# An mLSTM whose gate rows reach all partitions through memory and not through selector products

## The chip, the cores and the metric

The kernel runs on one core of a Trainium2 chip. The metric is device time in microseconds (us) of one execution; the kernel before has a median of 1518.31 us over three runs.

## The reference, cut to what matters

Two layers, each a mixer and a mixture of experts, on 512 tokens of width 1024. The mixer has two branches that read the same modulated rows, an mLSTM and a windowed attention. The part of the mLSTM that matters here:

```
# per head (4 heads, keys of 64, values of 128), causal, over 512 tokens
i, f      = gate columns of the input projection
b         = cumsum(log_sigmoid(f))
# state form, chunk by chunk, with a running maximum m (the stabilizer)
decay     = exp(b_last + m - m_new)
C_new     = decay * C + fresh * C_loc
# output of a token t of a chunk
W[s, t]   = exp(i_s - b_s + b_t - m_t)  for s <= t, else 0
num       = (W * (q k^T / 8)) v  +  exp(b_t + m - m_t) * (q / 8) C
out       = sigmoid(o) * rmsnorm(num / max(|den|, ...)) * w_mnorm
```

The kernel takes chunks of 128 tokens, so there are four of them, cc = 0 to 3.

## The kernel before

Large products run on TensorE (PE) in three passes each: every weight chunk is split into a high part (`wh`, by ScalarE, ACT) and a low part (`wl`, by VectorE, DVE), and the rows into `hh` and `hl`; a `unit` of the input projection is 24 products of 128x512. The units are v, the mLSTM's q and k (with a convolution `cv` on DVE and a silu `qk` on ACT), o (tiles `tok`, later `so`), the attention's `qa`, and so on. The pieces of the mLSTM are put between these units: `ml_prep` after 5 units of v and o, `ml_qi` and `ml_a(0)` between the units of o, then for each chunk `ml_b`, `ml_c`, `ml_a` of the next chunk, and `ml_d`.

The three gate rows are computed with one head per partition, on 4 partitions: `Mm` (4x512, the stabilizer), `inn` (4x512, the factor of the carried state) and `dec` (4x4, the decay of the state). They are needed on all 128 partitions. Before, a product with a 0/1 matrix does that: `sel` (4 x 4 x 128) and `sel2` (4 x 2 x 128), built by `selectors` in each layer. `ml_prep` makes `decp` and copies it to `decb`; `ml_qi` makes `innb` and multiplies q with it into `qi`; `ml_a` makes `mlW`, four blocks of 128x128, each a product of `sel` with `Mm` plus a product of `identb` (a bf16 identity) with `maskbig`, a 128x128 tile that is 1e30 above the diagonal. ACT then takes the exponential of `mlW` into `mlWs`, DVE multiplies it with the scores `mlS` into `mlSW`, and PE uses that in `mlN`. `ml_c` ends in `hm`, which `ml_d` turns on PE (`hmT`).

Every engine takes its instructions in the order of its own list. A list scheduler makes these lists from the program when the kernel is built, by its own estimates; so a change at one place may move instructions elsewhere. Weights come by the queue of SyncE (SP) into a ring of buffers (`raw`); among them is the modulation's weight `w_ada`, which DVE adds up into `acc` (`Ada.emit`), one 1 MB chunk in two instructions. A chunk's load starts when the instruction that read the buffer's former content has ended. GpSimd (POOL) has a DMA queue of its own, for small loads, for `bscr` and `brev` (a relative-position bias that goes to memory and is read back broadcast) and for gathers.

## Time and profile before

| | |
|---|---|
| runs | 1517.87, 1518.31, 1520.58 us; median 1518.31 us |
| profiled execution | its span from first to last instruction, 1523.3 us, is the one time known of it |
| span against the median | 5.0 us (0.33%) longer |
| PE | 1447.8 us busy (95%), 88% of the chain that ended last |
| DVE, ACT, POOL | 1094.8 us (72%), 759.6 us (50%), 220.3 us (14%) busy |
| the mLSTM in time | layer 0 from about 76 to 170 us, layer 1 from about 797 to 905 us of the span |

A view by windows gives busy time of each engine in a stretch and the clock granted to TensorE there; 1.00 is 2.4 GHz and 0.5 is 1.2 GHz. A row of the timeline gives start, duration, engine, line, operation, output and inputs, shape and count, and in square brackets how long the engine had been idle and what ended that. Products are pipelined, so one is issued before the last has ended, and the distance of two starts says more than a duration.

### The profile page before, as it was taken

To read this page: it belongs to the slowest core of one execution; us is meant where nothing else is said; L and a number is where in the kernel's file an instruction comes from. 1 tells how busy PE (TensorE), PEld (TensorE's weight loads), DVE (VectorE), ACT (ScalarE), POOL (GpSimd) and SP (SyncE) were. 2 spreads that over 40 slices of the span, in tenths; PEclk is the share of its full clock that TensorE was granted. 3 is DMA by queue.
4 is the path that set the end of the run, shared out by engine and by line. 5 is a ranking of instruction groups with operands and counts; after the bars stand their busy time and mean duration, and the time that the engine had idled before them with its cause. 6 is when DMAs were issued, how large, how long until landed. Compare 5 with 4: busy or idle time off the path is not lost.

```text
span 1523.3 us, 18682 instructions
## 1 busy us (share of the span) xinstructions
PE 1447.8 (95%) x6551; PEld 1085.9 (71%) x6551; DVE 1094.8 (72%) x2011; ACT 759.6 (50%) x1276; POOL 220.3 (14%) x266
## 2 busy tenths in 40 slices
PE   3999999999979999999899999999997999999995
PEld 2877777778867677677577777777886767767753
DVE  6776666767679777687766646656867977778757
ACT  4354444544356566566355334544434656656643
POOL 6500010010131111110230000001003111111023
PEclk9998999999989999999999899999998999999998
DMA  9564474575669999994735334446566999999582
GB/s 330 204 197 139 156 259 139 194 212 207 229 238 339 364 354 357 351 369 168 284 129 163 113 96 134 149 148 163 204 242 229 332 357 355 350 358 370 198 312 96
DMA packets 167779, 365.09 MB, mean 240 GB/s; under 512 B 11830, under 2 KB 42798, under 8 KB 167417
## 3 DMA queue, kind: packets, MB, share of 16 engines
q1 hardware_dynamic: 152928, 327.71, 62.2%
q0 software_dynamic: 14032, 33.93, 6.5%
q10 hardware_dynamic: 712, 2.14, 0.4%
q8 instruction: 55, 0.90, 0.2%
q14 instruction: 52, 0.42, 0.1%
HBM read 348.89 MB, written 29.41 MB: 248 GB/s over the span
## 4 chain that ended last, share of the span: by engine, by line
PE 88%; DVE 7%; issue 1%; DMA 1%; ACT 1%; another core or an unknown queue 0%; POOL 0%; SPq 0%; DVEq 0%; ACTq 0%; POOLq 0%
PE down L1449 9%; PE winT L112 7%; PE winT L113 7%; PE winT L114 7%; PE gate L114 4%; PE gate L112 4%; PE gate L113 4%; PE up L113 4%; PE up L114 4%; PE up L112 4%; PE out L112 2%; PE out L114 2%; PE out L113 2%; PE tok L114 2%; PE PV L909 2%; PE sc L867 2%
## 5 line engine op out<-in xcount | busy, mean ns | idle before, releaser
L1397 ACT CAST wh<-raw 128x1024 fp32r<-128x1024 f32 x248 | 258.2, 1049 | 214.5 <-PE gate L114 166.9
L1398 DVE TENSOR_TENSOR wl<-raw,wh 128x1024 fp32r<-128x1024 f32 x248 | 299.4, 1221 | 68.0 <-ACT wh L1397 64.4
L112 PE MATMUL winT<-hh,wh 128*128 128x512 f32 x432 | 177.3, 411 | 0.0
L113 PE MATMUL winT<-hl,wh 128*128 128x512 f32 x432 | 173.5, 402 | 0.0
L114 PE MATMUL winT<-hh,wl 128*128 128x512 f32 x432 | 173.0, 401 | 0.0
L1449 PE MATMUL down<-raw,aT 128*128 128x512 f32 x320 | 141.2, 593 | 3.0 <-ACT aT L1432 3.0
L479 ACT CAST wh<-raw 128x1024 fp32r<-128x1024 f32 (+1 forms) x59 | 54.4, 930 | 144.3 <-PE winT L113 99.2
L274 DVE SCALAR_TENSOR_TENSOR acc<-raw,cs,acc 128x1024 f32<-128x1024 f32 x70 | 89.6, 1280 | 35.3 <-DMA raw<-in_w_ada_dram 34.6
L112 PE MATMUL gate<-wh,XTh 128*128 128x512 f32 x256 | 109.9, 429 | 3.3 <-ACT XTh L1389 2.6
L1449 PEld LDWEIGHTS down<-raw,aT 128*128 128x128 f32 x320 | 59.2, 190 | 69.9 <-issue 65.5
L112 PEld LDWEIGHTS winT<-hh,wh 128*128 128x128 f32 x432 | 83.2, 193 | 29.9 <-issue 10.5
L113 PE MATMUL gate<-wl,XTh 128*128 128x512 f32 x256 | 103.1, 403 | 0.5 <-DVE wl L1398 0.5
L113 PE MATMUL up<-wl,XTh 128*128 128x512 f32 x256 | 101.5, 397 | 0.8 <-DVE wl L1398 0.8
L114 PE MATMUL gate<-wh,XTl 128*128 128x512 f32 x256 | 101.6, 397 | 0.2
L112 PE MATMUL up<-wh,XTh 128*128 128x512 f32 x256 | 101.2, 395 | 0.0
L114 PE MATMUL up<-wh,XTl 128*128 128x512 f32 x256 | 101.1, 395 | 0.0
L114 PEld LDWEIGHTS winT<-hh,wl 128*128 128x128 f32 x432 | 83.1, 192 | 19.8
L113 PEld LDWEIGHTS winT<-hl,wh 128*128 128x128 f32 x432 | 83.0, 192 | 18.1 <-DVE hl L459 0.3
L480 DVE TENSOR_TENSOR wl<-raw,wh 128x1024 fp32r<-128x1024 f32 (+1 forms) x57 | 60.7, 1067 | 44.1 <-ACT wh L479 43.8
L1358 POOL DMA_INDIRECT X<-h2d,gidx x30 | 38.9, 1296 | 281.8 <-PE XT L1370 258.8
L1451 DVE TENSOR_TENSOR Y<-down,g 128x512 f32<-128x512 f32 x60 | 40.4, 687 | 50.8 <-PE down L1449 50.8
L1452 POOL DMA_INDIRECT y2d<-Y,slot x30 | 37.8, 1261 | 225.9 <-DVE Y L1451 180.4
(490 smaller groups left out, 3053.7 us busy)
## 6 DMA issues: line engine op xcount, KB each, us to landing
raw<-in_w_down_e_dram SPq DMA_DIRECT2D x64, 1024.0 KB, 7.7
raw<-in_w_gate_e_dram SPq DMA_DIRECT2D x62, 1024.0 KB, 8.1
raw<-in_w_up_e_dram SPq DMA_DIRECT2D x62, 1024.0 KB, 8.5
raw<-in_w_ada_dram SPq DMA_DIRECT2D x40, 1024.0 KB, 5.3
raw<-in_w_in_dram SPq DMA_DIRECT2D x30, 1024.0 KB, 6.2
sch<-in_w_ada_dram SPq DMA_DIRECT2D x32, 256.0 KB, 6.3
raw<-in_w_out_dram SPq DMA_DIRECT2D x8, 1024.0 KB, 5.1
yk<-y2d SPq DMA_DIRECT2D x8, 1024.0 KB, 15.0
```

The lines of the kernel that those rows point to most:

```text
L112: T.matmul(o, lh, rh, start=start, stop=False)
L113: T.matmul(o, lh, rl, start=False, stop=False)
L114: return T.matmul(o, ll, rh, start=False, stop=stop)
L274: V.scalar_tensor_tensor(self.acc, ch[:, a], cs[:, kb:kb + 1], self.acc, op0=OP.mult, op1=OP.add)
L479: A.copy(wh[:, :, a:b], src)
L480: (G if "first" in st else V).tensor_sub(wl[:, :, a:b], src, wh[:, :, a:b])
L1358: G.indirect_dma_start(out=X[e % 2], out_offset=None, in_=h2d[l], in_offset=bass.IndirectOffsetOnAxis(ap=gidx0[:, e - 1:e] if e < 3 else g ...
L1397: A.copy(wh, src)
L1398: stt["split"] = E.tensor_sub(wl, src, wh)
L1449: T.matmul(pd[q], aT[:, fb], wd[fb // 2][:, fb % 2, q * 512:(q + 1) * 512], start=fb == 0, stop=fb == 3)
L1451: V.tensor_mul(Y[:, q * 512:(q + 1) * 512], pd[q], g2[:, q * 512:(q + 1) * 512])
L1452: stt["put"] = G.indirect_dma_start(out=y2d, out_offset=bass.IndirectOffsetOnAxis(ap=slot[:, e:e + 1], axis=0), in_=Y, in_offset=None, bou ...
```

## The change

The selectors, `identb` and the three kinds of broadcast product go. The rows are written to memory by POOL's queue as soon as they are computed (`mld[l]`, 8 x 512: rows 0 to 3 `Mm`, rows 4 to 7 `inn`; `mdd[l]`, 4 x 4) and read back, on the same queue, with each row repeated: two tiles `qb` (128x512, heads 2j and 2j+1 on 64 partitions each), four tiles `mb` (one for each chunk, all four heads on all partitions) and the two halves of `decb`. `ml_qi` multiplies q into `qb` in place. `ml_a` adds `maskbig` to `mb` on DVE, and ACT's exponential reads `mb`. The six tiles take buffers in SBUF; the banks of PSUM that `innb`, `decp` and `mlW` took are free. The rest of the diff removes comments.

```
+    mld = [dr.tile([8, S], F32, name=f"mld{l}") for l in range(NL)]
+    mdd = [dr.tile([4, 4], F32, name=f"mdd{l}") for l in range(NL)]
...
-    identb = con.tile([128, 128], BF, name="identb")
...
-        V.tensor_scalar(identb, jp, 0.0, None, op0=OP.is_equal)
...
-        sel = mp.tile([4, 4, 128], F32, name="sel", bufs=1)
-        sel2 = mp.tile([4, 2, 128], F32, name="sel2", bufs=1)
...
+        def rows(t, offset, ap):
+            return bass.AP(tensor=t.tensor, offset=t.offset + offset, ap=ap)
...
             V.tensor_sub(inn, mpv[:, :, None].to_broadcast([4, 4, 128]), Mm)
+            G.dma_start(mld[l][0:4], Mm)
             A.activation(inn, inn, AF.Exp)
             V.tensor_scalar(inn, inn, 0.125, None, op0=OP.mult)
+            G.dma_start(mld[l][4:8], inn)
...
             A.activation(dec, dec, AF.Exp)
-            st.update(RT=RT, Mm=Mm, inn=inn, dec=dec)
-
-        # token-major v and o
+            G.dma_start(mdd[l], dec)
+            st.update(RT=RT)
+
+            for j in range(2):
+                st["qb", j] = t5("qb")
+                G.dma_start(st["qb", j], rows(mld[l], (4 + 2 * j) * 512, [[512, 2], [0, 64], [1, 512]]))
+            for cc in range(4):
+                st["mb", cc] = t5("mb")
+                G.dma_start(st["mb", cc].rearrange("p (h k) -> p h k", h=4),
+                            rows(mld[l], cc * 128, [[0, 128], [512, 4], [1, 128]]))
+            for j in range(2):
+                G.dma_start(decb[:, j], rows(mdd[l], 8 * j, [[4, 2], [0, 64], [1, 4]]))
...
-        def selectors():
-            seli = t5("seli", I32)[0:4]
-            G.iota(seli.rearrange("k (h m) -> k h m", h=4), pattern=[[1, 4], [0, 128]], base=0, channel_multiplier=-1)
-            V.tensor_scalar(sel.rearrange("k h m -> k (h m)"), seli, 0.0, None, op0=OP.is_equal)
...
-            p = ps("decp")
-            for j in range(2):
-                T.matmul(p[:, j * 4:j * 4 + 4], sel2[:, j], st["dec"], start=True, stop=True)
-            V.tensor_copy(decb.rearrange("p a b -> p (a b)"), p[:, :8])
 
         def ml_qi(j):
-            p = ps("innb")
-            T.matmul(p, sel2[:, j], st["inn"].rearrange("k a b -> k (a b)"), start=True, stop=True)
-            qi[j] = t5(f"qi{j}")
-            V.tensor_mul(qi[j], p, qkT[j])
+            qi[j] = st["qb", j]
+            V.tensor_mul(qi[j], qi[j], qkT[j])
...
-            w_ = ps("mlW")
+            w_ = st["mb", cc]
...
-            for h in range(4):
-                T.matmul(w_[:, h * 128:(h + 1) * 128], sel[:, h], st["Mm"][:, cc, :], start=True, stop=False)
-                T.matmul(w_[:, h * 128:(h + 1) * 128], identb, maskbig, start=False, stop=True)
+            w4 = w_.rearrange("p (h k) -> p h k", h=4)
+            V.tensor_tensor(w4, w4, maskbig[:, None, :].to_broadcast([128, 4, 128]), op=OP.add)
```

The lists of the engines move as well. On **POOL in layer 0**, between the clearing of the gates' weight tiles (`wl`, `wh`, which every program has at 50 us) and the bias, there stood before:

```order
L531 MEMSET wh 128x1024
L153 DMA pr_673<-in_b_ada_dram 48x128
L154 DMA pr_673<-in_w_norm_dram 8x128
L155 DMA pr_673<-in_w_norm_dram 8x128
L156 DMA pr_673<-in_conv_w_dram 16x128
L157 DMA pr_673<-in_conv_b_dram 4x128
L225 IOTA antid 128x128
L231 MEMSET Fb 8x384
```

and now stands:

```order
L528 MEMSET wh 128x1024
L570 DMA mld_122<-Mm 4x512
L581 DMA mdd_124<-dec 4x4
L573 DMA mld_122<-inn 4x512
L592 DMA decb<-mdd_124 128x1x4 x2
L586 DMA qb<-mld_122 128x1x512 x2
L589 DMA mb<-mld_122 128x4x128 x4
L152 DMA pr_685<-in_b_ada_dram 48x128
```

The eleven DMAs of the rows stand ahead of the next layer's column parameters (`pr`), `antid`, the 32 copies of the bias and `bscr` and `brev`, all of which now wait until the rows have been computed.

On **DVE in layer 0**, behind the low part of the second half of o's first weights (`wl`), up to that of o's last half, there stood before (`acc` is `w_ada`'s sum, `cv` the convolution of k):

```order
L589 TENSOR_TENSOR wl_889<-raw_886,wh_888 128x1024
L272 TENSOR_SCALAR acc_927<-raw_928,cs_88 128x1024
L274 SCALAR_TENSOR_TENSOR acc_927<-raw_928,cs_88,acc_927 128x1024
L518 SCALAR_TENSOR_TENSOR cv_839<-winT_814,pc0_99,cv_839 128x509
L518 SCALAR_TENSOR_TENSOR cv_839<-winT_814,pc0_99,cv_839 128x510
L753 COPY Ttok_728<-RTt_932 128x48
L518 SCALAR_TENSOR_TENSOR cv_839<-winT_814,pc0_99,cv_839 128x511
L758 COPY decb_729<-decp_938 128x8
L589 TENSOR_TENSOR wl_943<-raw_886,wh_942 128x1024
L274 SCALAR_TENSOR_TENSOR acc_927<-raw_1011,cs_88,acc_927 128x1024
```

and now, in two pieces with two more steps of the first `cv` between them (a tile's number is its own in each program, but `raw_1011` is the same chunk in both, and `raw_1110` here is `raw_1118` there):

```order
L757 TENSOR_TENSOR qb_671<-qb_671,qk0_583 128x512
L271 TENSOR_SCALAR acc_937<-raw_938,cs_88 128x1024
L757 TENSOR_TENSOR qb_673<-qb_673,qk1_596 128x512
L273 SCALAR_TENSOR_TENSOR acc_937<-raw_938,cs_88,acc_937 128x1024
L768 TENSOR_TENSOR mb_675<-mb_675,maskbig_134 128x512
L768 TENSOR_TENSOR mb_677<-mb_677,maskbig_134 128x512
L768 TENSOR_TENSOR mb_679<-mb_679,maskbig_134 128x512
L225 TENSOR_SCALAR antid_691<-antid_691 128x128
L768 TENSOR_TENSOR mb_681<-mb_681,maskbig_134 128x512
L273 SCALAR_TENSOR_TENSOR acc_937<-raw_1011,cs_88,acc_937 128x1024 x2
L515 SCALAR_TENSOR_TENSOR cv_849<-winT_824,pc0_99,cv_849 128x509
```

```order
L515 SCALAR_TENSOR_TENSOR cv_849<-winT_824,pc0_99,cv_849 128x511
L273 SCALAR_TENSOR_TENSOR acc_937<-raw_1110,cs_88,acc_937 128x1024
L752 COPY Ttok_182<-RTt_942 128x48
L273 SCALAR_TENSOR_TENSOR acc_937<-raw_1110,cs_88,acc_937 128x1024
L515 SCALAR_TENSOR_TENSOR cv_885<-winT_860,pc0_99,cv_885 128x509
L515 SCALAR_TENSOR_TENSOR cv_885<-winT_860,pc0_99,cv_885 128x510
L605 TENSOR_TENSOR wl_949<-raw_896,wh_948 128x1024
L515 SCALAR_TENSOR_TENSOR cv_885<-winT_860,pc0_99,cv_885 128x511
```

All products with the rows now stand in one block ahead of both convolutions of k (`cv_849`, `cv_885`), of `Ttok` and of the low part of o's last quarter (`wl_949`, before `wl_943`). Two chunks of `w_ada` stand between them where one stood. The load of `raw_1011` is issued only when the instruction on `raw_938` behind the second `qb` has run, as before; that of the next chunk only when both on `raw_1011` have run, where before it waited for `wl_943`.

On **DVE in layer 0, around the end of chunk 0** (`mlr` and `nwt` are the steps of the inverse root in `ml_c`, `hm` its result), there stood before:

```order
L376 SCALAR_TENSOR_TENSOR nwt_1151<-nwt_1151,dd_1137 128x4
L377 SCALAR_TENSOR_TENSOR mlr_1149<-nwt_1151,mlr_1149 128x4
L840 SCALAR_TENSOR_TENSOR hm_1138<-mlN0_1122,mlr_1149,so0_1078 128x128
L840 SCALAR_TENSOR_TENSOR hm_1138<-mlN1_1123,mlr_1149,so0_1078 128x128
L840 SCALAR_TENSOR_TENSOR hm_1138<-mlN0_1122,mlr_1149,so0_1078 128x128
L840 SCALAR_TENSOR_TENSOR hm_1138<-mlN1_1123,mlr_1149,so0_1078 128x128
L480 TENSOR_TENSOR wl_1322<-raw_1198,wh_1321 128x8x64 x2
```

and now:

```order
L477 TENSOR_TENSOR wl_1298<-raw_1182,wh_1297 128x8x64
L375 SCALAR_TENSOR_TENSOR nwt_1143<-nwt_1143,dd_1129 128x4
L477 TENSOR_TENSOR wl_1298<-raw_1182,wh_1297 128x8x64
L376 SCALAR_TENSOR_TENSOR mlr_1141<-nwt_1143,mlr_1141 128x4
L374 TENSOR_TENSOR nwt_1143<-mlr_1141 128x4
L375 SCALAR_TENSOR_TENSOR nwt_1143<-nwt_1143,dd_1129 128x4
L376 SCALAR_TENSOR_TENSOR mlr_1141<-nwt_1143,mlr_1141 128x4
L832 SCALAR_TENSOR_TENSOR hm_1130<-mlN0_1114,mlr_1141,so0_1070 128x128
```

The two `wl` parts of the next unit of qa, whose buffers come free when the first unit of qa has ended on PE, stood behind `hm` and now stand ahead of it. PE's list still has `hmT` of chunk 0 right behind that first unit of qa, so it waits there for `hm`.

## Rows read from the trace of the kernel before

**Rows 1.** The page: the span, the engines' busy time (share of the span, instructions), and the chain that ended last by engine.

```profile
span 1523.3 us, 18682 instructions
...
PE 1447.8 (95%) x6551; PEld 1085.9 (71%) x6551; DVE 1094.8 (72%) x2011; ACT 759.6 (50%) x1276; POOL 220.3 (14%) x266
...
PE 88%; DVE 7%; issue 1%; DMA 1%; ACT 1%; another core or an unknown queue 0%; POOL 0%; SPq 0%; DVEq 0%; ACTq 0%; POOLq 0%
```

**Rows 2.** Groups of PE's instructions by line and shape over the whole span, the four that the change removes: count, busy time, mean ns of one, idle time before them.

```profile
L775 PE MATMUL mlW<-Mm,sel 4*128 4x128 f32 x64 | 16.0, 331 | 1.7 <-DVE qi L764 1.7
...
L776 PE MATMUL mlW<-maskbig,identb 128*128 128x128 bf16 x32 | 7.5, 233 | 0.0
...
L762 PE MATMUL innb<-inn,sel 4*128 4x512 f32 x8 | 4.0, 613 | 0.0
...
L757 PE MATMUL decp<-dec,sel 4*128 4x4 f32 x8 | 1.2, 253 | 0.0
```

**Rows 3.** Timeline of PE in layer 1, from `decp` to the first `mlW` block; each removed block is followed by the first product behind it.

```profile
826.84 0.60 PE L757 MATMUL decp<-dec,sel 4*128 4x4 f32 x4
827.37 0.50 PE L112 MATMUL tok<-wh,hh 128*128 128x512 f32 x1
...
833.15 1.98 PE L762 MATMUL innb<-inn,sel 4*128 4x512 f32 x4
835.06 0.51 PE L112 MATMUL tok<-wh,hh 128*128 128x512 f32 x1
...
843.03 0.48 PE L775 MATMUL mlW<-Mm,sel 4*128 4x128 f32 x2
...
845.24 0.39 PE L789 MATMUL ktok<-ident,qk 128*128 128x128 f32 x2
```

**Rows 4.** View by windows: stretch, its length, busy time (instructions) of PE, weight loads, DVE, ACT and POOL, then the granted clock, the DMA engines' share and GB/s. The first is in layer 0, the others in layer 1.

```profile
119.00:124.00 5.00, 5.00 (x16) 3.77 (x14) 4.44 (x10) 2.52 (x7) 0.00 (x0) 0.66 0.67 210
...
797.00:836.00 39.00, 39.00 (x167) 30.31 (x166) 27.96 (x40) 22.17 (x29) 0.00 (x0) 1.00 0.52 164
836.00:843.00 7.00, 7.00 (x30) 5.29 (x28) 3.03 (x3) 0.45 (x1) 0.00 (x0) 0.76 0.34 125
846.00:853.00 7.00, 7.00 (x27) 5.59 (x26) 3.62 (x9) 2.83 (x8) 0.00 (x0) 0.76 0.41 151
```

**Rows 5.** Timelines of DVE and PE in layer 1 around the end of chunk 0, and the end of `inn`.

```profile
811.50 0.42 DVE L568 TENSOR_SCALAR inn<-inn 4x512 f32<-4x512 f32 x1
...
861.14 1.12 DVE L840 SCALAR_TENSOR_TENSOR hm<-mlN,mlr,so 128x128 f32<-128x128 f32 x4
...
862.83 0.49 PE L848 MATMUL hmT<-ident,hm 128*128 128x128 f32 x3
```

**Rows 6.** Timeline of POOL: the bias's small write to memory and the reads that depend on it, 256 KB each.

```profile
60.55 0.53 POOL L241 DMA_DIRECT2D bscr<-Fb  x1 [0.29 <-POOL Fb L240]
62.92 2.91 POOL L245 DMA_DIRECT2D brev<-bscr  x4 [1.84 <-DMA bscr<-Fb]
```

**Rows 7.** Time from issue to landing of 256 KB reads on POOL's queue, least, median and most: first the four `brev`, then the two `wmn` (one row of memory repeated on all partitions); and, from the view of `brev`, its reader on PE with first and last start.

```profile
DMA to landing us min/median/max: 6.8/7.1/8.1
...
DMA to landing us min/median/max: 4.9/5.4/5.9
...
L253 PE MATMUL brevT<-brev,antid x8: 592/592/632, 185.6 to 188.6; 128*128 128x512 f32 x8
```

**Rows 8.** Timeline of DVE in layer 0, from `inn` to the last of `w_ada`'s instructions ahead of the scores.

```profile
90.97 0.41 DVE L568 TENSOR_SCALAR inn<-inn 4x512 f32<-4x512 f32 x1
...
102.24 1.22 DVE L589 TENSOR_TENSOR wl<-raw,wh 128x1024 fp32r<-128x1024 f32 x1
...
106.35 0.74 DVE L518 SCALAR_TENSOR_TENSOR cv<-winT,pc,cv 128x509 f32<-128x509 f32 x1
...
119.46 1.28 DVE L274 SCALAR_TENSOR_TENSOR acc<-raw,cs,acc 128x1024 f32<-128x1024 f32 x1 [1.59 <-DMA raw<-in_w_ada_dram]
```

**Rows 9.** Timeline of SP's queue in layer 0: the issue of the 1 MB chunk of `w_ada` that the last row of group 8 waits for.

```profile
114.36 0.38 SPq L100 DMA_DIRECT2D raw<-in_w_ada_dram  x1
```

**Rows 10.** Timeline of PE in layer 0 around o's last quarter.

```profile
104.20 1.98 PE L762 MATMUL innb<-inn,sel 4*128 4x512 f32 x4
...
111.89 0.71 PE L772 MATMUL mlS<-qk,qk 64*128 64x128 f32 x8
...
123.84 0.39 PE L114 MATMUL tok<-wh,hl 128*128 128x512 f32 x1
...
124.69 1.14 PE L804 MATMUL mlN<-v,mlSW 128*128 128x129 f32 x8
```

**Rows 11.** Timelines of PE, ACT and DVE in layer 0 at the end of qa's first unit: `hmT` of chunk 0, and the split of the next unit's weights.

```profile
136.56 0.27 PE L848 MATMUL hmT<-ident,hm 128*128 128x128 f32 x1
...
136.53 0.62 ACT L479 CAST wh<-raw 128x512 fp32r<-128x512 f32 x1 [5.73 <-PE winT L113]
...
134.37 0.16 DVE L377 SCALAR_TENSOR_TENSOR mlr<-nwt,mlr 128x4 f32<-128x4 f32 x1
134.57 1.13 DVE L840 SCALAR_TENSOR_TENSOR hm<-mlN,mlr,so 128x128 f32<-128x128 f32 x4
...
138.19 0.69 DVE L480 TENSOR_TENSOR wl<-raw,wh 128x512 fp32r<-128x512 f32 x1 [0.31 <-ACT wh L479]
```

**Rows 12.** The page's DMA queues: POOL's own, with packets, MB, and the time its packets took as a share of 16 engines' span.

```profile
q0 software_dynamic: 14032, 33.93, 6.5%
```

More of the change, by code (lines that the diff above doesn't have):

```diff
@@ L58 @@
 H2V = (0,)
-SELP = 1
 SPK = 6
@@ L536, in prep_gates @@
             return wh, wl
+        Ttok = mp.tile([128, 4, 3, 4], F32, name="Ttok", bufs=1)
+        decb = mp.tile([128, 2, 4], F32, name="decb", bufs=1)
+        def rows(t, offset, ap):
+            return bass.AP(tensor=t.tensor, offset=t.offset + offset, ap=ap)
         def body_gates(w):
@@ L730, in mixer @@
             unit()
-            if SELP == 1:
-                selectors()
         with tc.issue_after(last.ins):
@@ L735, in mixer @@
                 unit()
-            if l and SELP == 0:
-                selectors()
         if l == 0:
@@ L740, in mixer @@
             brs = bias_load(t5)
-        Ttok = mp.tile([128, 4, 3, 4], F32, name="Ttok", bufs=1)
-        decb = mp.tile([128, 2, 4], F32, name="decb", bufs=1)
         qi = {}
```

6 lines of the change are left out of this document (removed).

## The prediction

> **What bounds the kernel now.** I read the page first: PE is busy for 95% of the span and is 88% of the chain that ended last [rows 1]. So work taken from PE counts where PE runs without a gap, and a new wait counts only where PE comes to it. The groups by shape give what the change takes from PE: 16.0 + 7.5 + 4.0 + 1.2 = 28.7 us busy over both layers, with 1.7 us of idle time before it in all [rows 2]. Busy time counts overlapped products twice, so the price has to come from the distance of starts. In layer 1 PE goes from each removed block to the next product without a gap: `decp` takes 0.53 us (826.84 to 827.37), the two `innb` 1.91 (833.15 to 835.06), one `mlW` block 2.21 (843.03 to 845.24) [rows 3].
>
> The third view is the clock. In layer 1 TensorE is granted 1.00 (2.4 GHz) from 797 to 836 us, and 0.76 in the two stretches of 7 us that begin just behind the `innb` pair and the first `mlW` block [rows 4]: part of each ran at 1.2 GHz, and each lost some 7 x 0.24 = 1.7 us. The same is seen in layer 0, 0.66 from 119 to 124 us [rows 4].
>
> The timelines of DVE, POOL and SP tell when the rows exist and what a read from memory costs; they come with the parts that need them.
>
> **Part 1, PE in layer 1.** Removed: 0.53 + 1.91 + 4 x 2.21 = 11.3 us. One of the four `mlW` blocks is not gained in full. In chunk 0, PE arrives at `hmT` at 862.83, and DVE's four `hm` began at 861.14 (0.28 each) [rows 5]; DVE's chain starts with the end of `mlN`, ahead of the block, so if PE arrives 2.2 earlier, at 860.6, the first `hm` ends at 861.4 and PE waits 0.8. Rest: 10.5 us.
>
> The two stretches at 0.76 are worth up to 3.4 us. I take both as gone, since what is left at these places is a run of products at full rate (and 1.1 us of `mlS` and `ktok`); the bounds are 0 and, with the later slow stretches of the layer, 6.5 us. Layer 1: -14 us, bounds -10.5 and -17.
>
> Does the new path arrive in time there? `inn` ends at 811.92 [rows 5]. The small write and the first read that depends on it take 2.37 us from issue to issue (60.55 to 62.92, `bscr` and `brev`) [rows 6], so the first `qb` is issued at about 814.3. A 256 KB read on this queue lands 4.9 to 8.1 us after its issue [rows 7], 819.2 to 822.4. Behind it on DVE waits the low part of o's second quarter, which PE wants where `decp` stood, 826.84: 0.7 for the multiplication and 1.2 for `wl` end at 824.3 at the latest. Covered, by 2.5 us; if the cover is gone, each us of lateness is a us.
>
> **Part 2, PE in layer 0.** The rows come at the same place of the program, but DVE's list is another, as the section on the change shows: everything that PE needs next stands behind the first `qb`. `inn` is ready at 91.4 [rows 8]; with the 2.4 us of [rows 6], and the two `decb` reads ahead of it on POOL, the first `qb` is issued at about 94.2. Nearest row for its landing: `brev`, also a read of rows just written, 6.8 to 8.1 us; the `wmn` reads took 4.9 and 5.9 [rows 7]. SP's loads are in flight at the same time, so I take the lower `brev`: 101.0, with bounds 99.1 and 102.3.
>
> From that landing (q) on DVE, with 0.7 for a product of 128x512 (the 0.74 of `cv`), 0.7 for the first `acc` (one input less), 1.2 for the others (1.28, less the overlap of neighbours) and 1.2 for `wl` [rows 8]: two `qb` and two `acc`, q + 3.3. Only then is the load of the next `w_ada` chunk issued; from issue to use such a load takes 5.1 us (114.36 to 119.46) [rows 8, 9], q + 8.4, and the four additions of the mask (2.7 in all, landing at 0.73 us steps) lie under it. Two `acc`: q + 10.8, and the load of the next chunk starts there, q + 15.9; three `cv` lie under it. Two more `acc` and `Ttok`: q + 18.5. Two `cv`, `wl`, one `cv`: `wl` at q + 21.1, the last `cv` at q + 21.8, and ACT's silu 0.6 later. With q = 101.0 the last k is there at 123.4.
>
> PE gets to `mlS` at 111.89 - 0.53 - 1.91 = 109.4 [rows 3, 10]. It can do half the scores and then waits, for `wl` until 122.1 and for k until 123.4, and has 22 products of o left, at full clock 39.00 us / 167 = 0.234 each [rows 4], 5.1. With 0.4 for `mlS` and 0.6 for small products behind o (the last one of o starts at 123.84, `mlN` 0.85 later), `mlN` of chunk 0 starts at 129.5, where it started at 124.69 [rows 10]: 4.8 us late. After such a gap some products may run at 1.2 GHz, as they did from 119 to 124 [rows 4], 1.7 us. I take 5.5; the bounds are 3.0 (q = 99.1) and 8 (q = 102.3 and the slow clock).
>
> Chunk 0's end gets a second wait. PE's list has `hmT` behind the first unit of qa, ended at 136.56 before; `hm` was done by then (134.57 + 1.13) [rows 11]. Now the split of the next weights stands ahead of `hm`, and that split starts with the end of the unit: from ACT's 136.53 to the second `wl`'s end, 138.19 + 0.69, it takes 2.35 us [rows 11], then three or four small steps of 0.2 (`mlr` at 134.37, `hm` at 134.57) and the first `hm`, 0.3: 3.3 us of waiting. Against it stand three `mlW` blocks (the first one was counted in `mlN`'s start), 6.6 us.
>
> Layer 0: 5.5 + 3.3 - 6.6 = +2.2 us; bounds -0.5 (rows early) and +5.
>
> **Part 3, what costs nothing.** The building of the selectors, `identb` and `decb`'s copy go from DVE and POOL; no removed wait of PE hangs on them, so I count 0. On POOL the bias's write and read now follow the rows, from 54 us to about 110; its reader on PE starts at 185.6 [rows 7], so some 65 us hide it. If they did not, its 8 us of landing would be the price. In layer 1 the four additions (2.7 us of DVE) lie in front of `cv` and `wl` with the cover told above.
>
> A page of the Trainium skill prices the landing otherwise: "DMA: Bandwidth & Descriptors", section on the anatomy of one DMA on the GpSimd path, gives about 2.0 us fixed plus the bytes at 436 GB/s, so by an estimate from it 2.6 us for 256 KB. The reads here took 4.9 to 8.1 us [rows 7], in company of other loads; by the page q would be 96.8 and the forecast 4 us lower.
>
> **The sum.** -14 + 2.2 = -11.8 us. The profiled execution, 1523.3 [rows 1], would become 1511.5; the runs' median lies 5.0 below its own profile, so 1506.5 for the median, 0.8% faster. About 0.2% (3 us) is what a measurement of this kernel can tell from no change.
>
> **The rivals.**
>
> *Layer 0 costs nothing* (1492 us). If the reads land well ahead, by 92 us say, or if DVE's waits are shorter than the rows say, PE gains there too: 0.53 + 1.91 + 4 x 2.21 less 0.8, and the 1.7 of waiting before `mlW` [rows 2]: 12.5. With layer 1's 14 that is 26.5. For it: PE is the bound. Against it: `inn` itself is not ready before 91.4.
>
> *DVE becomes the bound* (1511 us). PE's gain in chunks 1 to 3 would end in waits for `hm`, as counted once above at 0.8 us. At 0.8 for each of the six others, 4.8 us less. Before, PE came 0.6 us after the last `hm` ended in layer 1 (862.83 against 862.26) [rows 5], so not much is spare.
>
> *Two of the sixteen DMA engines carry each `qb`* (1515 us). Its access pattern begins with a count of 2 (two heads, each 64 times), whereas that of `brev` begins with 128. If a transfer is divided by its first count, one engine has 64 rows of 2 KB to move and not 8. POOL's packets took 6.5% x 16 x 1523.3 / 14032 = 0.113 us each, at 2.4 KB [rows 1, 12]: 7.2 us against 0.9. `qb` lands 6.3 us later: layer 0 loses 6.3 us, and in layer 1 the cover of 2.5 to 5.7 us is used up, 2.7 lost on the middle. -11.8 + 9.0 = -2.8. No row shows a large read of this form. The Trainium skill has such a rule: "DMA: Bandwidth & Descriptors", section on why a DMA increments its semaphore by 16, says that the number of engines is the largest up to 16 that divides the first counts of both sides, and names an exception for some copies on this queue; no run here shows it.
>
> *The wait at the head of DVE's list costs more than PE's work* (1526 us, slower). DVE cannot pass over the first `qb`, and the convolutions, o's weights and SP's next loads hang behind it. Layer 0 has to lose 11.8 us more than counted: `qb` landing at 113 and not 101. It does if both reads go to the same two engines, 128 packets x 0.113 = 14.5 us behind 94.2 + 4: 112.7, or if SP's traffic halves the rate of two engines. In layer 1 the same puts `qb` at 832.8, and the low part of o's second quarter 8 us behind 826.84. Sum -11.8 + 11.7 + 8 = +8.
>
> **How the numbers follow.** Forecast 0.42; layer 0 free 0.14; DVE the bound 0.12; two engines 0.15; slower 0.17. The predicted time is the first, 1506.5; its own range is 1501 to 1513 (bounds -17 - 0.5 and -10.5 + 5). The range for 8 in 10 is 1493 to 1522: it leaves out about half of the first rival and half of the last. Faster by over 0.2%: 0.42 + 0.14 + 0.10 + half of two engines, less a little for what was not thought of, 0.70; within 0.2% 0.14; slower 0.16.
>
> **What would show it.** In the profile after: no `decp`, `innb`, `mlW`; in layer 1 the two stretches at 0.76 back near 1.00 and no wait of PE above 1 us ahead of `hmT`; in layer 0 PE idle some 13 us between 109 and 123, ended by `wl` and then by `qk`, and about 3 us at the first `hmT`; on DVE a wait for `qb` ending near 101, and two waits for `w_ada` chunks behind it. `qb` landing more than 10 us after its issue would show the DMA rivals. PE not idle at 115 would show the first rival. A wait of PE in layer 1 at o's second quarter would make the forecast wrong on the slow side.

## The result, and the profile after

The changed kernel takes 1534.85 us (median of four runs, 1534.03 to 1538.06) against 1519.44 us in the runs of the kernel before on the same chip: a ratio of 1.0098, 95% interval 1.0075 to 1.0120. It is 15.4 us, 1.0%, slower. The forecast of 1506.5 us was wrong, and its range, 1493 to 1522, does not hold the time. The profiled execution took 1534.03 us.

The page of the changed kernel, lines that answer to [rows 1, 12]:

```profile
span 1532.0 us, 18482 instructions
...
PE 1425.8 (93%) x6439; PEld 1070.3 (70%) x6439; DVE 1096.5 (72%) x2012; ACT 760.5 (50%) x1276; POOL 237.5 (16%) x282
...
q0 software_dynamic: 17104, 37.14, 7.5%
...
PE 78%; DVE 9%; DMA 5%; issue 4%; ACT 2%; POOL 1%; another core or an unknown queue 0%; DVEq 0%; SPq 0%; ACTq 0%; POOLq 0%
```

PE runs 112 instructions less, as many as the four groups of [rows 2] count. Its busy time is 22 us less than in [rows 1], but 14.5 less than in a second profile of the kernel before (1440.3 us, the first experiment), so the number of instructions is the surer sign. Its share of the chain that ended last fell from 88% to 78%: DVE, DMA and unexplained issue time took its place. PE now waits.

The profile of before that stands ahead of the prediction was a slower execution; that second one has a span of 1518.0 us, and stages are compared with that one. Starts of PE's instructions in us, out of the timelines of seven kernels (their experiments follow). `mlN(0)` is the first product of chunk 0, `hmT(3)` the turn of chunk 3, and `RTt` the turn of the gate rows just ahead of the place where `decp` stood; the last column is the distance from `RTt` to the last `hmT(3)`:

```
                         layer 0              layer 1
                    mlN(0)   hmT(3)     RTt     mlN(0)  hmT(3)   RTt to hmT(3)
before, again       127.09   179.82    827.58   852.31  897.60      70.0
changed             137.10   189.66    837.75   861.64  910.80      73.1
only mlW            129.76   177.76    826.07   847.11  895.01      68.9
  with hm first     129.18   177.46    825.87   846.90  886.33      60.5
changed, hm first
  in layer 1        139.14   193.27    841.69   866.31  905.69      64.0
bias first, spread  133.22   189.63    836.54   860.31  907.85      71.3
  mb later, hm first 128.91  182.60    831.04   849.28  890.09      59.1
```

Layer 0 lost 10.2 us (up to `RTt` of layer 1), and layer 1, which was to gain 14, lost 3.0. A single profile gives such a start only roughly: the changed kernel and the one with `hm` first in layer 1 have the same instructions in the same order on every engine up to this `RTt`, and theirs lie 3.9 us apart (837.75 and 841.69). Distances within a stage, like the last column, vary less than the starts. View by windows of the changed kernel, and then of the kernel before profiled again (columns as in [rows 4]):

```profile
100.00:150.00 50.00, 28.88 (x147) 21.60 (x145) 33.63 (x70) 18.51 (x39) 13.85 (x47) 0.76 0.62 182
850.00:900.00 50.00, 40.75 (x198) 31.20 (x197) 33.86 (x109) 20.60 (x62) 0.00 (x0) 0.83 0.46 148
```

```profile
100.00:150.00 50.00, 46.99 (x248) 34.84 (x247) 39.15 (x100) 20.66 (x52) 0.00 (x0) 0.93 0.60 185
850.00:900.00 50.00, 50.00 (x276) 38.72 (x275) 33.45 (x116) 19.84 (x65) 0.00 (x0) 1.00 0.27 86
```

PE idles 21.1 of the 50 us in layer 0 and 9.3 in layer 1, and in both stretches the granted clock is lower as well. The waits of PE in layer 0 of the changed kernel:

```profile
120.60 0.80 PE L765 MATMUL mlS<-qk,qk 64*128 64x128 f32 x4 [12.22 <-ACT qk L518]
122.80 0.47 PE L781 MATMUL ktok<-ident,qk 128*128 128x128 f32 x1 [1.40 <-DVE Ttok L752]
...
137.10 1.13 PE L796 MATMUL mlN<-v,mlSW 128*128 128x129 f32 x8 [1.40 <-DVE mlSW L775]
...
150.29 0.30 PE L840 MATMUL hmT<-ident,hm 128*128 128x128 f32 x1 [3.34 <-DVE hm L832]
```

k (`qk`) is late because DVE is. DVE's waits in layer 0, which answer to [rows 8]:

```profile
105.11 0.69 DVE L757 TENSOR_TENSOR qb<-qb,qk 128x512 f32<-128x512 f32 x1 [11.85 <-DMA qb<-mld]
...
113.71 2.60 DVE L273 SCALAR_TENSOR_TENSOR acc<-raw,cs,acc 128x1024 f32<-128x1024 f32 x2 [2.67 <-DMA raw<-in_w_ada_dram]
...
121.34 1.28 DVE L273 SCALAR_TENSOR_TENSOR acc<-raw,cs,acc 128x1024 f32<-128x1024 f32 x1 [2.80 <-DMA raw<-in_w_ada_dram]
```

POOL's timeline answers to [rows 6]; each row's bracket is what its DMA waited for:

```profile
92.28 1.61 POOL L586 DMA_DIRECT2D qb<-mld  x2
...
100.34 0.53 POOL L153 DMA_DIRECT2D pr<-in_w_norm_dram  x1 [2.64 <-DMA decb<-mdd]
105.36 0.53 POOL L154 DMA_DIRECT2D pr<-in_w_norm_dram  x1 [4.49 <-DMA qb<-mld]
...
108.29 0.26 POOL L224 IOTA antid<- 128x128 f32 x1
...
121.77 2.88 POOL L244 DMA_DIRECT2D brev<-bscr  x4 [4.45 <-DMA bscr<-Fb]
```

The parameter loads wait for landings of the row reads ahead of them, `antid`'s numbers come only at 108.29, and the 1 MB of `brev` is read at 121.77, where it was read at 62.92 [rows 6].

Layer 1 of the changed kernel, DVE's two decisive waits, SP's issue of the chunk that the second one is for, and then PE's waits (answering to [rows 5]):

```profile
835.53 0.69 DVE L757 TENSOR_TENSOR qb<-qb,qk 128x512 f32<-128x512 f32 x1 [6.08 <-DMA qb<-mld]
...
869.49 0.76 DVE L271 TENSOR_SCALAR acc<-raw,cs 128x1024 f32<-128x1024 f32 x1 [2.73 <-DMA raw<-in_w_ada_dram]
```

```profile
863.23 0.37 SPq L99 DMA_DIRECT2D raw<-in_w_ada_dram  x1
```

```profile
853.66 0.49 PE L765 MATMUL mlS<-qk,qk 64*128 64x128 f32 x4 [3.65 <-ACT qk L518]
...
875.65 0.45 PE L840 MATMUL hmT<-ident,hm 128*128 128x128 f32 x1 [5.60 <-DVE hm L832]
```

### The profile page after: what moved, and what is told of

Read it like the earlier page. It is cut to its first block, busy times and chain, and to the rows that moved or that the text cites. A ratio compares the mean times of both kernels' runs of the same rounds, so it can differ in the third digit from the quotient of the medians.

```text
span 1532.0 us, 18482 instructions
## 1 busy us (share of the span) xinstructions
PE 1425.8 (93%) x6439; PEld 1070.3 (70%) x6439; DVE 1096.5 (72%) x2012; ACT 760.5 (50%) x1276; POOL 237.5 (16%) x282
## 4 chain that ended last, share of the span: by engine, by line
PE 78%; DVE 9%; DMA 5%; issue 4%; ACT 2%; POOL 1%; another core or an unknown queue 0%; DVEq 0%; SPq 0%; ACTq 0%; POOLq 0%
PE down L1441 9%; PE winT L111 6%; PE winT L112 5%; PE winT L113 5%; PE gate L113 4%; PE gate L111 4%; PE gate L112 4%; PE up L112 4%; PE up L113 4%; PE up L111 4%; DMA raw<-in_w_ada_dram 3%; PE out L111 2%; PE out L113 2%; PE out L112 2%; PE PV L901 2%
## 5 line engine op out<-in xcount | busy, mean ns | idle before, releaser
L1390 DVE TENSOR_TENSOR wl<-raw,wh 128x1024 fp32r<-128x1024 f32 x248 | 299.5, 1222 | 68.0 <-ACT wh L1389 63.8
L111 PEld LDWEIGHTS winT<-hh,wh 128*128 128x128 f32 x432 | 81.8, 189 | 29.5 <-issue 10.5
```

The lines of the kernel that those rows point to most:

```text
L111: T.matmul(o, lh, rh, start=start, stop=False)
L1390: stt["split"] = E.tensor_sub(wl, src, wh)
```

## The experiments

### The kernel before again

No edit. 

> The kernel before, unchanged, for a second profile. Its first profile had a span of 1523.3 us while its runs have a median of 1519.4; the kernel after had a span 2.0 us below its own run's time. If the first profile of before was a slow execution, the second spans about 1517 to 1518 us, and places where it is faster than the first are not places of the change. If the spans agree within 1 us, the 8.7 us between the two profiles and the 15.4 us between the runs contradict each other.

1519.83 us, span 1518.0. TensorE's clock from 845 to 855 us is 1.00; of the two slow stretches of [rows 4] only the first is there. So the second was a property of that one execution.

### The landing of qb alone, its consumers' place, or another engine

Three kernels, each the whole change with one edit (each build makes its own lists). First, each `qb` and `decb` as two reads of 64 partitions:

```
-G.dma_start(st["qb", j], rows(mld[l], (4 + 2 * j) * 512, [[512, 2], [0, 64], [1, 512]]))
+for h in range(2):
+    G.dma_start(st["qb", j][h * 64:(h + 1) * 64], rows(mld[l], (4 + 2 * j + h) * 512, [[0, 64], [1, 512]]))
```

> The kernel after with each qb and each decb read as two reads of 64 partitions, whose access pattern begins with a count of 64 and not 2; twelve reads and not eight. Theory A (two of the sixteen DMA engines carry each qb, so it lands late): qb lands 5 to 7 us after its issue in both layers and not 8 to 13; layer 0 gains 4 to 6 us, layer 1 2 to 3; time 1525 to 1529 us. Theory B (the reads are late because of other traffic or of the queue, however they are divided): qb still lands 8 to 13 us after its issue and the two more issues on the queue add about 1.5 us; time 1534 to 1537 us.

Second, DVE's order: `qb` behind o's last low part, chunk 0's mask behind k's last `cv`, each other mask behind `mlSW` of the chunk before; for that, `ml_qi` also moves behind o's units in the program.

```
+with tc.issue_after(st["o3"].ins):
     V.tensor_mul(qi[j], qi[j], qkT[j])
...
+with tc.issue_after(st["cv"].ins if cc == 0 else st["sw"].ins):
     V.tensor_tensor(w4, w4, maskbig[...], op=OP.add)
```

> The kernel after with the same reads, but DVE's two products with qb ordered behind the low part of o's last quarter, the first mask addition behind the convolution of k, and the others behind the scores of the chunk before. Theory C (the loss is the wait at the head of DVE's list, and what is queued behind it): no wait of PE over 2 us in o in either layer, mlN of chunk 0 some 12 us earlier in layer 0 and 5 earlier in layer 1 than in the kernel after; the waits at hmT stay; time 1503 to 1510 us, faster than the kernel before. Rival (the rows are late for PE itself, or DVE's added work makes it the bound): PE waits at mlN or at mlS for the rows instead; time 1518 us or more.

Third, `qb`'s products and the mask's additions on POOL (`V.` becomes `G.` in these two lines).

> The kernel after with the same reads, but the two products with qb and the four mask additions on POOL. Theory C: DVE waits for no row, PE has no wait over 2 us in o; time 1501 to 1510 us. Rival (DVE's added 5 us of work or the reads themselves set the time): 1518 us or more. If it is 3 us or more slower than the ordered variant on DVE, POOL's instructions of 128x512, 1.3 to 2.5 us each, are late or hold up DVE.

Measured: 1536.13 us (ratio 1.0093, 1.0060 to 1.0126), 1539.73 (1.0116, 1.0077 to 1.0155) and 1548.58 (1.0172, 1.0135 to 1.0209). None is clearly faster than the changed kernel (1.0098). DVE's waits in the first and in the second:

```profile
101.25 0.69 DVE L759 TENSOR_TENSOR qb<-qb,qk 128x512 f32<-128x512 f32 x1 [4.27 <-DMA qb<-mld]
...
119.16 1.28 DVE L273 SCALAR_TENSOR_TENSOR acc<-raw,cs,acc 128x1024 f32<-128x1024 f32 x1 [5.30 <-DMA raw<-in_w_ada_dram]
```

```profile
109.22 0.38 DVE L225 TENSOR_SCALAR antid<-antid 128x128 f32<-128x128 f32 x1 [10.85 <-POOL antid L224]
...
113.95 2.61 DVE L273 SCALAR_TENSOR_TENSOR acc<-raw,cs,acc 128x1024 f32<-128x1024 f32 x2 [4.35 <-DMA raw<-in_w_ada_dram]
```

Spread reads come 3.9 us sooner, the two `w_ada` chunks behind them only 2.5 and 2.2 (111.25 and 119.16, against 113.71 and 121.34). And this build puts the first step of k's first `cv` behind the second chunk (120.36), where the changed kernel has all three ahead of it (from 116.23); PE waits 16.82 us for k and not 12.22. So this run doesn't show what sooner reads alone are worth. With the products out of the way, DVE waits at the same time of day for `antid`, which hangs on POOL's list. My first theory, that the wait for `qb` at the head of DVE's list is the whole loss, fell: take one late thing away and the next stands behind it.

### One half of the change at a time

Only the `mlW` rows by memory (`sel2`, `innb`, `decp` put back), and only the state-factor and decay rows (`sel`, `identb`, `mlW` put back).

> Only the stabilizer rows (mlW) go through memory; the state-factor and decay rows keep their products with selectors. Mm is written at about 85.4 us in layer 0, 4 us before inn, and its four reads (128 partitions first) are spread over all 16 DMA engines. DVE's four additions of the mask stand ahead of antid and of the first pair of w_ada steps, and antid's IOTA stands behind the four reads on GpSimd. Theory A (in layer 0 everything behind the first wait at the head of DVE's list is late by that wait, and the chain of w_ada loads behind it makes PE idle): the rows land near 95 and the parameter reads and the IOTA run by about 100, so the wait is 10 us shorter than in the changed kernel; some 5 us lost in layer 0 against some 17 gained by the removed mlW products, 1508 to 1516. Rival B (what costs is the two-engine transfer of qb): without qb nothing is lost, 1500 to 1506. Rival C (the four reads of 256 KB crowd SP's weight loads, whatever else there is): as slow as the changed kernel, 1528 to 1540, with waits for w_ada of 4 us and more on DVE.

> Only the state-factor and decay rows go through memory; the mlW products with selectors stay, so PE's work is some 2.4 us a layer less than before. Theory A: qb still stands at the head of DVE's list ahead of the w_ada pairs and both of these ahead of the first cv of k: qb lands near 103, the loads are 8 us late in layer 0 and 3 in layer 1, 1525 to 1535. Rival B (two-engine qb is what costs): the same time, since qb is left; 1525 to 1535. Rival C (crowding by the four mb reads): without them nothing is late, 1512 to 1520.

1518.60 us (0.9969, 0.9954 to 0.9984) and 1542.99 (1.0119, 1.0099 to 1.0140). The half that takes most of PE's work is a little faster than before; the one with `qb` loses at least as much as the whole (the intervals overlap), and its time is above what any of the three theories gave it. There the load of the second `w_ada` pair met `brev`'s reads, 108.47 (SP's issue) to 116.25, 7.8 us; POOL's row, then DVE's:

```profile
107.73 2.95 POOL L246 DMA_DIRECT2D brev<-bscr  x4 [5.17 <-DMA bscr<-Fb]
```

```profile
116.25 2.60 DVE L275 SCALAR_TENSOR_TENSOR acc<-raw,cs,acc 128x1024 f32<-128x1024 f32 x2 [7.80 <-DMA raw<-in_w_ada_dram]
```

The half with `mlW` falls between theories A and C. Why it gains only 0.3% is seen in layer 1: DVE, PE and the clock of that kernel, then DVE in the kernel before, again.

```profile
852.98 0.75 DVE L271 TENSOR_SCALAR acc<-raw,cs 128x1024 f32<-128x1024 f32 x1 [2.61 <-DMA raw<-in_w_ada_dram]
```

```profile
859.15 0.45 PE L849 MATMUL hmT<-ident,hm 128*128 128x128 f32 x1 [3.78 <-DVE hm L841]
```

```profile
860.00:865.00 5.00, 5.00 (x17) 3.34 (x15) 1.07 (x3) 1.21 (x5) 0.00 (x0) 0.50 0.99 334
865.00:870.00 5.00, 5.00 (x24) 3.84 (x25) 2.89 (x18) 2.15 (x9) 0.00 (x0) 0.50 0.08 31
```

```profile
854.88 0.74 DVE L272 TENSOR_SCALAR acc<-raw,cs 128x1024 f32<-128x1024 f32 x1
```

SP's load of this chunk was issued at much the same time in both (846.85, and 845.78 before):

```profile
846.85 0.37 SPq L99 DMA_DIRECT2D raw<-in_w_ada_dram  x1
```

```profile
845.78 0.37 SPq L100 DMA_DIRECT2D raw<-in_w_ada_dram  x1
```

Its reader on DVE, which stands ahead of chunk 0's `hm` in both programs, found DVE free 4.5 us earlier (852.98 less 2.61, against 854.88), because `mlN` came earlier (847.11 against 852.31), and now had to wait; so did `hm` and PE. After 3.78 us without work PE ran at 1.2 GHz for the ten microseconds shown.

### The bias first, and the order on DVE

Both kernels write and read the rows behind the bias's work on POOL in layer 0 and keep the consumers late. The second also puts the second `w_ada` pair behind k's first `cv`, and that `cv` right behind the first pair.

```
+*brs, last_read = bias_load(t5)
+with tc.issue_after(last_read.ins):
+    st["read"]()          # the rows' writes and reads
```

```
+with tc.issue_after(st["cv", 2].ins) if (l, i) == (0, 8) else ExitStack():
     ada_emit(1)
```

> The whole change, but GpSimd builds the bias before the rows' writes and reads, as in the kernel before (antid's IOTA waits for nothing), and on DVE the qb products stand behind o's last low part and the mask's additions behind k's last cv or the chunk before. The second w_ada pair still stands ahead of k's first cv, and its load runs while the rows are read. Theory A without crowding: DVE waits for nothing ahead of the cv but a 5 us load, PE's idle time between 100 and 150 us falls from 21 to about 5 us; 1505 to 1512. Rival C (crowding): the w_ada load that is issued near 98 lands at 113 as in the kernel with late consumers, the first cv of k is late all the same, 1530 to 1540.

> As the run before, and the second w_ada pair of layer 0 stands behind k's first cv, so that no instruction ahead of PE's next needs anything that is loaded while the rows are read. Theory A and rival C both say that layer 0's PE then does not wait for cv (under 3 us idle between 100 and 125): 1500 to 1510. If it is still above 1520, the cause lies neither in DVE's order nor in the loads behind it, but in something that the rows themselves set (their late landing at mlSW, or DVE's and GpSimd's additional work).

1534.53 us (1.0077, 1.0054 to 1.0099) and 1524.80 (1.0026, 1.0005 to 1.0047). In the first, `antid` waits for nothing, and the wait stands at the load, as the crowding rival said; in the second PE's wait for k falls to 5.29 us, not under the 3 expected, and the work put off falls on chunk 0's end:

```profile
117.72 2.60 DVE L273 SCALAR_TENSOR_TENSOR acc<-raw,cs,acc 128x1024 f32<-128x1024 f32 x2 [16.90 <-DMA raw<-in_w_ada_dram]
```

```profile
142.32 0.66 PE L853 MATMUL hmT<-ident,hm 128*128 128x128 f32 x2 [8.31 <-DVE hm L845]
```

```profile
135.00:140.00 5.00, 0.00 (x0) 0.00 (x0) 5.00 (x21) 1.88 (x6) 0.00 (x0) 0.70 0.36 127
```

From 135 to 140 us DVE is busy without a gap and PE has nothing. The gain that both theories gave the second kernel, to 1510 or less, did not come: its DVE became the bound there.

### The two-engine reads, and the volume of the reads

Only `qb`'s half, each `qb` as two reads; and the whole change with that and the bias first.

> As the run with only the state-factor and decay rows in memory (1543 us; its first qb came 12.0 us after its issue and DVE waited 11.1 us for it), but each qb is read as two reads of 64 partitions, which spread over all 16 DMA engines. Theory A (qb's transfer by two engines is what costs there): qb lands 5 to 6 us after its issue, DVE's wait falls to about 5 us, the w_ada load behind it is issued some 6 us earlier and no longer meets the reads of brev (4 x 256 KB), 1518 to 1528. Rival (the order on DVE and the moved bias cost the time, however fast qb is): 1536 to 1545.

> The whole change, with the bias on GpSimd ahead of the rows' writes and reads and each qb as two reads of 64 partitions; DVE's order is left to the build. Theory A (two-engine reads, and the moved bias): layer 0's PE idle time between 100 and 150 us falls from 21 to 6 to 10 us, 1514 to 1522. Rival C (1.5 MB of reads of rows, mb's 1 MB above all, share the DMA engines with SP's weight loads, so that w_ada loads issued near 98 take 10 us and more): 1526 to 1536.

1533.32 us (1.0093, 1.0059 to 1.0127), between the two expectations, and 1528.41 (1.0048, 1.0021 to 1.0074). Against `qb` in one read the first is 9.7 us less by the medians, but the two ran beside different runs of the kernel before; by the ratios to these (1.0119 and 1.0093) it is 4 us, and the intervals overlap. The page's packet count and the landing times in the view of `qb`, first in one read, then in two:

```profile
DMA packets 170146, 366.20 MB, mean 237 GB/s; under 512 B 13925, under 2 KB 44901, under 8 KB 169784
...
DMA to landing us min/median/max: 8.1/10.5/13.6
```

```profile
DMA packets 168417, 366.17 MB, mean 239 GB/s; under 512 B 12197, under 2 KB 43173, under 8 KB 168056
...
DMA to landing us min/median/max: 2.9/6.2/9.5
```

The four `qb` of one read each bring 1728 packets under 512 B more. In the records of the DMA packets each `qb` is 64 of 4096 B, and the small ones of the changed kernel are of 8 B for the most part: 896 per layer, which is 32 for each of 14 engines and each `qb`. The records name no engine, but in layer 1 of the half with one read two of the 4096 B packets are under way at a time while the first `qb` goes alone, and four for the most part once the second has joined; of the spread reads up to 16 are. So two engines carry the 256 KB of a `qb`. That the others send the 8 B packets as fillers is read from their number. The Trainium skill's rule ("DMA: Bandwidth & Descriptors", section on why a DMA increments its semaphore by 16: as many engines, up to 16, as divide the first counts of both sides) gives two for this pattern; the trace agrees.

But that is some 4 to 10 us of the 18 to 24 that this half loses (by ratios and by medians), and the whole change with spread reads is still slower than before. DVE, SP's issue and the windows in the whole one:

```profile
111.58 1.28 DVE L273 SCALAR_TENSOR_TENSOR acc<-raw,cs,acc 128x1024 f32<-128x1024 f32 x1 [11.07 <-DMA raw<-in_w_ada_dram]
```

```profile
99.30 15.76 SPq L99 DMA_DIRECT2D raw<-in_w_ada_dram  x2
```

```profile
100.00:105.00 5.00, 5.00 (x25) 4.08 (x24) 0.50 (x1) 1.05 (x1) 1.37 (x6) 1.00 1.07 288
```

The chunk of `w_ada` is used 12.3 us after its issue (99.30 to 111.58); before, such a load took 5.1 [rows 8, 9]. The DMA engines' share is 1.07 meanwhile: on the mean of the engines there is work all the time. That is the rival of this run, crowding.

### What repairs it

The half with `mlW` alone, with the `w_ada` pair of the unit behind chunk 0 put after `hm` on DVE; and the same with the bias first.

```
+with tc.issue_after(st["hml", 0].ins) if l in (0, 1) and i == 14 else ExitStack():
     ada_emit(1)
```

> As the run with only the mlW rows in memory (1518.6 us), but the w_ada pair that is emitted with the unit after chunk 0 stands behind chunk 0's last hm on DVE, in both layers. In layer 1 that pair's load held hm up: DVE idle 2.61 us for it, PE idle 3.78 at hmT, and then TensorE at 0.50 from 860 to 870 us. Theory (a PE wait of some 4 us costs about as much again in clock): the wait falls under 1.5 us, the granted clock of 860 to 870 is 1.00, 5 to 8 us gained: 1510 to 1514. Rival (DVE's chain from mlN to hm is longer than PE's work between them in any case, since the mlW block that covered it is gone): wait still above 2 us and the clock still falls, 1515 to 1519.

> As the run before, and the bias on GpSimd goes ahead of the mlW rows' write and reads in layer 0. With only the mlW rows moved, the w_ada load of layer 0 that was issued at 102.9 us was used at 108.4 after DVE had waited 4.84 us, while the parameter and bias transfers ran; antid's additions waited behind the masks. If these collisions cost layer 0 what it lost there (mlN of chunk 0 2.7 us later than before), 2 to 4 us are gained on the run before: 1507 to 1511. Rival: the rows are then read later (the write waits for nothing, but the w_ada pair stands ahead of or behind the mask's additions by another order), no gain: 1511 to 1516.

1509.20 us (0.9931, 0.9903 to 0.9958) and 1512.99 (0.9952, 0.9930 to 0.9974). In the first, PE has no wait at layer 1's first `hmT`, and the clock behind it is whole:

```profile
855.01 0.60 PE L851 MATMUL hmT<-ident,hm 128*128 128x128 f32 x4
```

```profile
860.00:865.00 5.00, 5.00 (x23) 4.09 (x24) 4.72 (x27) 0.84 (x3) 0.00 (x0) 1.00 1.00 364
```

Layer 1 takes 60.5 us from `RTt` to the last `hmT` instead of 68.9: 8.5 us for a wait of 3.78. The bias first did not help, as that run's rival said: `inn` is ready 2.8 us later there (the subtraction at 90.39 against 87.58; the cause stays open, and the two executions of the same list named above lie 1.6 apart at that place), SP's load comes as much later, and both instructions of the second `w_ada` pair now stand ahead of `Ttok`, for which PE waits 6.16 us where it waited 1.03. DVE's first wait there:

```profile
103.36 0.75 DVE L271 TENSOR_SCALAR acc<-raw,cs 128x1024 f32<-128x1024 f32 x1 [6.37 <-DMA raw<-in_w_ada_dram]
```

Last, the whole change with everything that had been found: bias first, `qb` in two reads, `hm` first, and three of the four `mb` reads held back by a small copy on POOL from what the chunk before produces; and the changed kernel with nothing but `hm` first in layer 1.

```
+def read_mb(cc, gate=None):
+    st["mb", cc] = t5("mb")
+    if gate is not None:
+        G.tensor_copy(st["mb", cc][:, 0:2], gate)
+    return G.dma_start(...)
...
+if cc < 3:
+    read_mb(cc + 1, st["SW", cc - 1][:, 2, 0:2] if cc else Ttok[:, 0, 0, 0:2])
```

> The whole change, with the bias first on GpSimd, each qb as two reads, chunk 0's w_ada pair behind hm on DVE, and only the first of the four mb reads next to qb's: each of the others waits on GpSimd for a small copy from what chunk before it produces (Ttok, then mlSW), so 0.75 MB of reads leave the stretch in which SP loads the w_ada chunk. Theory C (the reads' volume on the DMA engines is what makes that chunk late: 12.3 us from issue to use in the run with bias first and spread qb, at a DMA share of 0.98 to 1.07): the chunk is used 7 to 9 us after its issue, PE's wait for k falls from 11.4 to 5 to 7 us, and layer 1 loses no time at hmT: 1508 to 1518. Rival (the chunk is late for another reason, such as its own buffer): still 11 us and more, 1520 to 1526, the gain being layer 1's alone.

> The changed kernel as it is, but in layer 1 the w_ada pair that stood ahead of chunk 0's hm on DVE stands behind it. Theory: PE's wait of 5.6 us at hmT in layer 1 falls under 2 us, and with it the low clock behind it (0.83 from 850 to 900 us); as much as in the kernel with only the mlW rows, 8 to 10 us: 1525 to 1528. Rival: the other waits of layer 1 (qk, 3.65 us, and qb on DVE, 6.1 us) leave the clock low and hm late anyway: 1530 to 1535.

1512.60 us (0.9940, 0.9916 to 0.9964) and 1526.31 (1.0024, 1.0010 to 1.0037), both inside what the theories gave. DVE, SP and PE of the first, PE's wait for k in the build with bias first and spread `qb` that it is held against, and PE at layer 1's first `hmT` in the second, without a wait:

```profile
108.14 1.28 DVE L273 SCALAR_TENSOR_TENSOR acc<-raw,cs,acc 128x1024 f32<-128x1024 f32 x1 [8.42 <-DMA raw<-in_w_ada_dram]
```

```profile
98.33 13.95 SPq L99 DMA_DIRECT2D raw<-in_w_ada_dram  x2
```

```profile
115.38 0.80 PE L778 MATMUL mlS<-qk,qk 64*128 64x128 f32 x4 [6.45 <-ACT qk L518]
```

```profile
121.10 0.80 PE L773 MATMUL mlS<-qk,qk 64*128 64x128 f32 x4 [11.39 <-ACT qk L518]
```

```profile
874.40 0.60 PE L842 MATMUL hmT<-ident,hm 128*128 128x128 f32 x4
```

The chunk is used 9.8 us after its issue, a little more than the 7 to 9 expected. With the bias first, the time from issue to use of the same chunk is then 16.9 us (two-engine `qb`, all reads: 100.85, SP's issue, to 117.72), 12.3 (`qb` spread) and 9.8 (0.75 MB of reads moved away too), against 5.1 with no row reads. These are different builds, so the steps are not pure; their direction is what the volume and the two full engines would give. PE's wait for k fell by 4.9 us, and not all of it is the load: the masks left DVE's list ahead of k's first `cv` with their reads, and from the chunk's use to the end of that `cv` it is 5.2 us where it was 7.5. The best kernel measured is the half with `mlW` and `hm` first, 10.8 us (0.7%) faster than before; the mended whole change is within its interval.

## Why the prediction was wrong, point by point

In the terms of the sum, layer 0 was put at +2.2 us and came at +10.2, and layer 1 was put at -14 and came at +3.0. The larger miss is layer 1's. The changed kernel spends 73.1 us there from `RTt` to the last `hmT`: 9.3 of waiting (3.65 for k and 5.60 for `hm`) and 63.8 of work at a clock of 0.88, work that the mended kernel does in 57.7 us at 1.00.

- **What the change takes from PE** was right: the 112 products are gone, and in the mended kernel layer 1 needs 59.1 us from `RTt` to the last `hmT` where it needed 70.0. Of these 11.0 us some 1.4 are the clock (1.00 against 0.98 over the stretch; 70.0 x 0.02, an estimate), and 1.3 of new waiting stand against them; the sum without the clock said 10.5.
- **"No wait of PE above 1 us ahead of `hmT`" in layer 1, term 0.8 us, failed**: 5.60 measured. I moved DVE's chain with PE's, but the load of the `w_ada` chunk inside it starts when DVE's last reader of the buffer has ended (a `wl`, at 863.20; SP's issue follows at 863.23), and not sooner because PE has less to do. From `mlN` to `hm` DVE took 8.5 us before, 11.5 in the half with `mlW` (2.61 of it this wait) and 13.5 in the changed kernel (2.73 of it; the rest of that growth is the order of DVE's other steps, which no run takes apart). It costs more than its size: putting the pairs behind `hm` gave 9.1 us in the changed kernel (73.1 to 64.0) and 8.5 in the half.
- **The cover of 2.5 us for the first `qb` in layer 1 failed.** I had it land 7.3 to 10.5 us after `inn`'s end; it was used 12.2 after it (823.38 by DVE's timeline, to 835.53). DVE's 6.08 us, and 2.46 more for the next `w_ada` pair (at 847.04), became a wait of 3.65 for k on PE.
- **The clock term, 3.4 us gained, had the wrong sign.** One of its two stretches was not there in the second profile of before, and the new waits brought new ones: 0.83 from 850 to 900 us. In the mended kernel, where PE waits 1.3 us in all there, the clock of layer 1 is 1.00; so the term hung on there being no new wait.
- **Layer 0, landing of `qb` at 101.0 (bounds 99.1 to 102.3)**: 105.1. It was issued sooner than I put it (92.28 and not 94.2), so from issue to use it took 12.8 us where I took 6.8. The 6.0 between them are close to the 6.3 that I gave the two-engine case, which I had set apart as a rival. I chose the lower `brev` row, a read of another pattern. What hangs behind was sized right: the next two `w_ada` chunks at q + 8.4 and q + 15.9, measured q + 8.6 and q + 16.2; the wait at `hmT` 3.3, measured 3.34.
- **Layer 0, "some products may run at 1.2 GHz", 1.7 us**, was too small. `mlN` was put at q + 28.5 and came at q + 32.0. 1.40 of it is a wait for `mlSW`, in no term of mine; for the rest the rows of that stretch in the changed kernel show a slow clock, PE having been idle since 108:

```profile
115.00:120.00 5.00, 0.00 (x0) 0.00 (x0) 3.44 (x4) 1.37 (x2) 2.02 (x5) 0.50 0.48 154
...
125.00:130.00 5.00, 3.26 (x10) 2.13 (x11) 5.00 (x7) 2.08 (x3) 0.00 (x0) 0.50 0.99 288
```

- **Three `mlW` blocks less, -6.6 us**, were not seen: from `mlN(0)` to the last `hmT` of layer 0 it is 52.6 us, before 52.7. The 3.3 of the wait and the clock of that stretch (0.90, before 0.97: some 3.7 us, an estimate from 52.6 x 0.07) ate them.
- **Part 3, "costs nothing", failed.** The cover I named, 65 us, was that of the bias's reader on PE. I overlooked that `antid`, in the same moved work, has a reader on DVE ahead of the `w_ada` pair (10.85 us of waiting once `qb` is out of its way), and that 1 MB of `brev` reads moved into the stretch in which SP loads weights.
- **The rivals.** Nearest came *the wait at the head of DVE's list* (1526 us), which already counted the two engines: it put layer 0 at +13.9 and layer 1 at -6, measured +10.2 and +3.0, so it too had no wait above 0.8 us at `hmT` in layer 1. *Layer 0 costs nothing* is out, as PE is idle at 115. *DVE becomes the bound* did not show in the changed kernel, where no `hmT` of chunks 1 to 3 waits; in the mended one two do for more than 1 us (2.99 and 1.06). Two of these sums were off: the loss on the middle in the two-engine case is 2.2 and not 2.7, and layer 0's gain in the first rival 12.2 and not 12.5; neither moves its time by more than 0.5 us. That the four `mb` reads slow the weight loads was in none of them. The estimate of 2.6 us for a read, by the Trainium skill's "DMA: Bandwidth & Descriptors", section on the anatomy of one DMA on the GpSimd path, was met by no read of the rows of 256 KB: the quickest `mb` of the half with `mlW` alone took 3.7, the four `qb` of the changed kernel 8.2 to 13.5.

Settled are the wait for `hm` with its clock, that a `qb` goes out on two engines and lands late, and that the four edits of the mended kernel together take the loss away. Not settled is what each is worth in layer 0: every build has its own lists there, and the spread reads brought nothing in the whole change by themselves. That 0.75 MB of reads less makes the chunk come sooner (12.3 to 9.8 us) is likely, with the masks moved in the same run. The 3.5 us of layer 0's loss that are left up to `RTt` in the mended kernel are no more than two executions of one list differ there.

## What to carry to other kernels

When work moves from the engine that bounds to a trip through memory, list what stands behind each landing on every in-order list, DMA queues included, and count all bytes that this puts beside other loads; a load that was just in time does not come sooner because the engine ahead of it has less to do. A wait of PE has a second price, the clock: here 3.8 us of waiting cost 8.5 and 5.6 cost 9.1. And put the chunk that can wait behind the chain that cannot: one line of order was worth about as much in layer 1 (8.5 to 9.1 us) as four `mlW` blocks (8.8).
